# Decode cache values moved behind the state-space product of the output projection

## The chip, the cores and the metric

One core of a Trainium2 chip runs the whole kernel. The time is device microseconds from one execution to the end of it; a run's number is that of the core. The engines are TensorE (PE; its weight loads are PEld), VectorE (DVE), ScalarE (ACT), GpSimd (POOL) and SyncE (SP), whose queue issues nearly all DMAs in order. Each engine works its instructions off in the order in which they stand in the built program.

## The reference, cut to what matters

One step of a one-layer hybrid decoder: 1024 prompt tokens and 8 decode tokens (T = 1032 columns), model width 1024. Three attention patterns (dilated windows, 8 heads of 64 each) are merged per position by their softmax denominators; a Mamba-2 branch gives 1024 more columns, gated by silu(z) and normalised; one output projection takes both.

```python
def merge_patterns(outs, lses):
    alpha = jax.nn.softmax(jnp.stack(lses, axis=0), axis=0)
    o = sum(alpha[g][..., None] * outs[g] for g in range(N_PATTERNS))
    return o.reshape(o.shape[:-2] + (ATTN_OUT,))
...
    # decode tokens: each pattern's probabilities times the cached values
    o = jnp.einsum('bthk,btkhd->bthd', p, sel[:, :, :, 1].astype(jnp.float32)) / den
...
    ssm = ssd_gate_out(y, xs, z, d_skip, ssd_norm_w)
    mix = jnp.concatenate([attn.astype(xn.dtype), ssm.astype(xn.dtype)], axis=-1) @ w_out
```

The moved block computes that einsum over 128 cached keys for 8 decode tokens and 3 patterns, already weighted for the merge, and adds the new keys' part.

## The kernel before

Activations stand transposed, 128 rows of features by T columns, and the columns are cut into three chunks of 344 (688 to 1031, with the 8 decode tokens, is the last). Every large product is made of three fp32r products (high by high, high by low, low by high); load_w loads a 512 KB weight tile wr, ScalarE casts it to wh, and DVE (or GpSimd) subtracts to get wl. gemm does one weight tile against the chunks of cc: unit issues 8 x 3 matmuls of 128x344 per chunk into a PSUM tile g, about 7.5 us for two chunks.

A scheduler places the instructions of each engine when the program is built. The blocks carry priorities (the context prio): "evac" goes first, then "w" (weight loads and casts), "side", "late", and "main" (the matmuls of unit) last; inside one kind the order of the text counts. What has been placed on an engine runs in that order on the chip.

The stages around the change, in time:

- The z projection (the loop over k with gemm of w_in[36 + k], 831 to 976 us). Per k: 72 matmuls into g, ScalarE copies g to zt (L893), silu, DVE multiplies into yg (L901), ScalarE squares into zt (L906), and GpSimd adds the squares up in acc (L908, k = 1 to 6). k = 7's squares go straight to a matmul.
- Beside it, as "late" work: the merge weights. The softmax statistics come back as sn (L809), wg and wo are worked out, transposed (wtp), copied to wts (L834) and stored to w_d (L835).
- Then the merge of the prompt's attention, 16 rounds (4 quarters of the prompt by 4 head pairs, L838 to L849): load nt (384 KB, L840) and wt (2 broadcasts of 96 KB, L843), GpSimd multiplies (L845), DVE adds twice (L846, L847), ScalarE casts into ah (L848), DVE subtracts into al (L849). The pool mgp has two buffers of nt and of wt.
- Also "late" in the z stage: the decode block (L852 to L880). For each of 8 tokens, three loads of cached values (cvt, 128x512, 256 KB each, L861), three multiplies by probabilities (L864; pattern 0 on DVE, patterns 1 and 2 on GpSimd), two DVE adds (L867, L868), one matmul with a selector column (L869; sums over the 128 keys into nps, two records each). Then osb (copy, L871), four transposes (L874), adds into dat, and the last 8 columns of ah and al. The pool cvp has five buffers, so a token's three and two of the next fit.
- The state-space part of the output projection for chunks 0 and 1: the scaled rows sh and sl (L914, L915), the row sums (ptp, L921 and L922), then m = 0 and 1 in one loop (L945), then m = 2 to 7 by gemm with cc = (0, 1) (L953), evacuated by DVE into mix.
- The attention part, chunk 0 first (unit with ah, al and the pair of weights from load_pair, L959 on). The weights of m = 0, 1 and m = 2, 3 are kept in a pool wrs (wah0, wal0, wah2, wal2); later pairs are loaded again per chunk. Chunk 1 follows, and chunk 2, which alone reads the decode columns of ah and al.

The pools of the right-hand side of SBUF form a stack: a pool opened after another was closed takes its space, and its first writer waits for the last reader of what lay there. Before, mgp and cvp lie beside each other, both are closed, and wrs is opened in their space.

Of the kernel before, what the change touches and what calls it, by code (L numbers as in the profile page):

```python
# [8 lines left out]
F32 = mybir.dt.float32  # L9
# [39 lines left out]
def trunk(tc, a, o):  # L49
# [62 lines left out]
    def after(ins, first):  # L112
        tc.add_manual_dep(ins.ins, first.ins.name,
                          mybir.DependencyInfo(mybir.DependencyClass.Sync, mybir.DependencyReason.DATA),
                          reason="order")

    def next_copy(ins):
        pace[1] += pace[0]
        if copies and pace[1] >= 1:
            pace[1] -= 1  # L120
            d, s = copies.pop()
            after(nc.sync.dma_start(out=d, in_=s), ins)
# [37 lines left out]
    def unit(ps, w, hs, ls, c, ch=CH):  # L160
        wh, wl = w
        c0, c1 = ch[c]
        n = len(hs)
        with prio("main"):
            for k in range(n):
                ws = slice(k * P, (k + 1) * P)
                for j, (x, y) in enumerate(((wh, hs[k]), (wl, hs[k]), (wh, ls[k]))):
                    nc.tensor.matmul(ps, x[:, ws], y[:, c0:c1], start=(k == 0 and j == 0),  # L168
                                     stop=(k == n - 1 and j == 2))

    gpools = [psg]
    ngp = [0]
# [8 lines left out]
    def gemm(src, cols, hs, ls, evac, cc=(0, 1, 2), share=False):  # L181
        w = load_w(src, cols, share)
        for c in cc:
            ps = gps()
            unit(ps, w, hs, ls, c)
            with prio("evac"):
                next_copy(evac(c, ps))

    def rms(src_ps, dst):
        nc.scalar.activation(out=dst, in_=src_ps, func=AF.Sqrt, bias=epst, scale=1.0 / D)  # L190
# [607 lines left out]
    rst = ExitStack()  # L798
    mgp = pool(rst, "mgp", 2, side="right")
    QT = 256  # L800
    cvp = pool(rst, "cvp", 5, side="right")
    ah = cap.tile([P, HP, T], F32R, name="ah")
    al = cap.tile([P, HP, T], F32R, name="al")

# [43 lines left out]
                nc.scalar.copy(ah[:, hp, qs], nt[:, 0])  # L848
                nc.vector.tensor_tensor(out=al[:, hp, qs], in0=nt[:, 0], in1=ah[:, hp, qs], op=ALU.subtract)  # L849


    with prio("late"):  # L852
        sel = cap.tile([P, NB * NB], F32, name="sel")
        nc.vector.memset(sel, 0.0)
        nc.vector.memset(sel[:, 0:NB * NB:NB + 1], 1.0)
        ops = att_ps("nps")
        for b in range(NB):
            vts = []
            for g in range(NG):
                vt = cvp.tile([P, 512], F32, tag="cv", name="cvt")  # L860
                nc.sync.dma_start(out=vt, in_=a[f"cache{g}"][b].rearrange("(k r) c -> r k c", r=DIL[g])[0, :, 512:1024])  # L861
                pw = dpt[:, g].rearrange("p h (x b) -> p b x h", b=NB)[:, b].unsqueeze(3)
                v4 = vt.rearrange("p (x h d) -> p x h d", x=HP, h=2)
                (nc.gpsimd if g else nc.vector).tensor_tensor(out=v4, in0=v4, in1=pw.to_broadcast([P, HP, 2, 64]),  # L864
                                                              op=ALU.mult)
                vts.append(vt)
            nc.vector.tensor_tensor(out=vts[0], in0=vts[0], in1=vts[1], op=ALU.add)  # L867
            nc.vector.tensor_tensor(out=vts[0], in0=vts[0], in1=vts[2], op=ALU.add)  # L868
            nc.tensor.matmul(ops[:NB], sel[:, b * NB:(b + 1) * NB], vts[0], start=(b == 0), stop=(b == NB - 1))  # L869
        osb = cvp.tile([NB, 512], F32, tag="cv", name="osb")  # L870
        nc.scalar.copy(osb, ops[:NB])  # L871
        otp = att_ps("nps")
        for hp in range(HP):
            nc.tensor.transpose(otp[:, hp * NB:(hp + 1) * NB], osb[:, hp * P:(hp + 1) * P], ident[:NB, :NB])  # L874
        nc.vector.tensor_tensor(out=dat, in0=otp[:, 0:HP * NB], in1=dnv[:, 0], op=ALU.add)
        for g in range(1, NG):
            nc.vector.tensor_tensor(out=dat, in0=dat, in1=dnv[:, g], op=ALU.add)
        dv = dat.rearrange("p (h b) -> p h b", h=HP)
        nc.scalar.copy(ah[:, :, S:T], dv)
        nc.vector.tensor_tensor(out=al[:, :, S:T], in0=dv, in1=ah[:, :, S:T], op=ALU.subtract)  # L880
    rst.close()


# [4 lines left out]
    for k in range(KT):  # L888
        zt = gp.tile([P, T], F32, tag="zt", name="zt")

        def ev(c, ps, zt=zt):
            c0, c1 = CH[c]
            return nc.scalar.copy(zt[:, c0:c1], ps)  # L893

        gemm(a["w_in"][36 + k], 1024, xh, xl, ev)
        with prio("side"):
            yt = mixp.tile([P, T], F32, tag="mix", name=f"yg{k}")
            nc.sync.dma_start(out=yt, in_=y_d[k])
        with prio("evac"):
            nc.scalar.activation(out=zt, in_=zt, func=AF.Silu)  # L900
            nc.vector.tensor_tensor(out=yt, in0=yt, in1=zt, op=ALU.mult)  # L901
            yg.append(yt)
            if k == 0:
                nc.scalar.activation(out=acc, in_=yt, func=AF.Square)
            else:
                nc.scalar.activation(out=zt, in_=yt, func=AF.Square)  # L906
                if k < KT - 1:
                    nc.gpsimd.tensor_tensor(out=acc, in0=acc, in1=zt, op=ALU.add)  # L908
    sh, sl = [], []
    with prio("evac"):  # L910
        for k in range(KT):
# [36 lines left out]
    with prio("evac"):  # L948
        for m in range(2):
            for c in range(2):  # L950
                ssm_ev(m)(c, pq[m][c])
    for m in range(2, KT):
        gemm(a["w_out"][m][:, 512:1536], 1024, sh, sl, ssm_ev(m), cc=(0, 1))  # L953
    ahs = [ah[:, k] for k in range(HP)]
    als = [al[:, k] for k in range(HP)]
    wrs = pool(right, "wrs", 1, side="right")
# [308 lines left out]
```

## Time and profile before

| | us |
|---|---|
| median of 3 runs | 1928.76 |
| lowest, highest | 1927.81, 1932.84 |
| the profiled execution | 1929.59 |
| its span (first to last instruction) | 1927.8 |
| TensorE busy in it | 1825.0 |
| decode block, first load to last matmul | 875.0 to 950.1 |
| last subtraction of the merge (al) | 1035.4 |
| attention part, first matmul | 1049.9 |

The profiled execution took 1.8 us more than its span, and 0.8 more than the median. In the rows below L-numbers are lines of the kernel before; "idle before" is the time that an engine stood still just before an instruction, with what released it. A timeline row may stand for several equal instructions (x2), and for SP its length counts the waiting within the row.

### The profile page before, as it was taken

To read this page: it belongs to the slowest core of one execution; us is meant where nothing else is said; L and a number is where in the kernel's file an instruction comes from. 1 tells how busy PE (TensorE), PEld (TensorE's weight loads), DVE (VectorE), ACT (ScalarE), POOL (GpSimd) and SP (SyncE) were. 2 spreads that over 40 slices of the span, in tenths; PEclk is the share of its full clock that TensorE was granted. 3 is DMA by queue.
4 is the path that set the end of the run, shared out by engine and by line. 5 is a ranking of instruction groups with operands and counts; after the bars stand their busy time and mean duration, and the time that the engine had idled before them with its cause. 6 is when DMAs were issued, how large, how long until landed. Compare 5 with 4: busy or idle time off the path is not lost. (4 is left out here: it accounts for less than half of the span.)

```text
span 1927.8 us, 29260 instructions
## 1 busy us (share of the span) xinstructions
PE 1825.0 (95%) x11727; PEld 1709.3 (89%) x11727; DVE 1014.0 (53%) x1896; ACT 739.2 (38%) x1388; POOL 394.5 (20%) x277
## 2 busy tenths in 40 slices
PE   8999989999999899998879989999999999999994
PEld 6999878888888798887679989999999999999993
DVE  6544676757764544455774896331333333333348
ACT  5543554545554455665242353222221112211242
POOL 0000244543232311133533342000000000000025
PEclk9999999999999999999889999999999999999997
DMA  4322333443334433464754454347433643366362
GB/s 162 122 95 86 119 108 112 137 128 107 104 115 136 156 100 110 142 237 137 178 154 133 147 168 132 109 150 249 133 115 130 240 164 131 105 202 207 115 247 88
DMA packets 125544, 275.26 MB, mean 143 GB/s; under 512 B 17616, under 2 KB 83632, under 8 KB 124000
## 3 DMA queue, kind: packets, MB, share of 16 engines
q1 hardware_dynamic: 125408, 273.39, 43.4%
q8 instruction: 92, 1.51, 0.3%
q14 instruction: 44, 0.36, 0.1%
HBM read 235.86 MB, written 125.47 MB: 187 GB/s over the span
## 5 line engine op out<-in xcount | busy, mean ns | idle before, releaser
L168 PE MATMUL g<-xh,wh 128*128 128x344 f32 x1344 | 443.7, 330 | 9.7 <-ACT zt L893 5.5
L168 PE MATMUL g<-xl,wh 128*128 128x344 f32 x1344 | 440.4, 328 | 1.5 <-DVE xl L222 1.5
L168 PE MATMUL g<-xh,wl 128*128 128x344 f32 x1344 | 439.0, 327 | 0.5 <-DVE wl L157 0.5
L168 PEld LDWEIGHTS g<-xh,wh 128*128 128x128 f32 x1344 | 255.8, 190 | 19.3 <-ACT zt L893 6.1
L168 PEld LDWEIGHTS g<-xh,wl 128*128 128x128 f32 x1344 | 256.2, 191 | 11.3 <-issue 9.9
L168 PEld LDWEIGHTS g<-xl,wh 128*128 128x128 f32 x1344 | 256.3, 191 | 10.4 <-issue 7.4
L157 DVE TENSOR_TENSOR wl<-wr,wh 128x1024 fp32r<-128x1024 f32 (+1 forms) x133 | 163.0, 1226 | 124.9 <-ACT wh L156 124.7
L156 ACT CAST wh<-wr 128x1024 fp32r<-128x1024 f32 (+1 forms) x133 | 134.4, 1011 | 214.5 <-PE g L168 128.8
L168 PE MATMUL pg<-fh,wl 128*128 128x344 f32 x504 | 161.8, 321 | 0.2 <-DVE wl L157 0.2
L168 PE MATMUL pg<-fl,wh 128*128 128x344 f32 x504 | 161.8, 321 | 0.0
L168 PE MATMUL pu<-fl,wh 128*128 128x344 f32 x504 | 161.6, 321 | 0.0
L168 PE MATMUL pu<-fh,wh 128*128 128x344 f32 x504 | 161.2, 320 | 0.0
L168 PE MATMUL pu<-fh,wl 128*128 128x344 f32 x504 | 160.8, 319 | 0.0
L168 PE MATMUL pg<-fh,wh 128*128 128x344 f32 x504 | 158.5, 322 | 0.0
L1110 POOL TENSOR_TENSOR ow<-wr,ow 128x512 fp32r<-128x512 f32 x8 | 11.1, 1407 | 674.9 <-ACT ow L1109 674.9
L168 PE MATMUL g<-hl,wh 128*128 128x344 f32 x432 | 138.0, 319 | 0.0
L168 PE MATMUL g<-hh,wl 128*128 128x344 f32 x432 | 137.6, 319 | 0.0
L168 PE MATMUL g<-hh,wh 128*128 128x344 f32 x432 | 137.3, 320 | 0.0
L230 DVE TENSOR_TENSOR u<-pu,rf 128x344 f32<-128x344 f32 x66 | 34.1, 516 | 195.5 <-PE pu L168 195.5
L650 ACT ACTIVATE sm<-sm,ngm 128x128 f32<-128x128 f32 (+1 forms) x192 | 84.9, 443 | 108.3 <-DVE ngm L646 106.2
L606 POOL TENSOR_TENSOR sw<-sw,sin 128x1032 f32<-128x1032 f32 x24 | 74.9, 3122 | 247.6 <-ACT sw L605 184.1
L1079 ACT CAST hh<-s 128x344 fp32r<-128x344 f32 x66 | 31.7, 480 | 199.4 <-DVE s L1078 197.3
(323 smaller groups left out, 3710.7 us busy)
## 6 DMA issues: line engine op xcount, KB each, us to landing
out_skv<-in_cache SPq DMA_DIRECT2D x64, 1023.5 KB, 5.3
wr<-in_w_in SPq DMA_DIRECT2D x56, 512.0 KB, 3.8
wr<-in_w_fin SPq DMA_DIRECT2D x44, 512.0 KB, 3.8
out_skv<-in_cache SPq DMA_DIRECT2D x16, 1022.0 KB, 5.5
wr<-in_w_out SPq DMA_DIRECT2D x24, 512.0 KB, 4.1
wr<-in_w_fout SPq DMA_DIRECT2D x24, 384.0 KB, 4.2
e<-cs_d SPq DMA_DIRECT2D x16, 512.0 KB, 3.9
n_d<-nh SPq DMA_DIRECT2D x12, 512.0 KB, 4.2
```

Source lines behind the costliest of these rows:

```text
L156: nc.scalar.copy(wh[:, :cols], wr[:, :cols])
L157: nc.vector.tensor_tensor(out=wl[:, :cols], in0=wr[:, :cols], in1=wh[:, :cols], op=ALU.subtract)
L168: nc.tensor.matmul(ps, x[:, ws], y[:, c0:c1], start=(k == 0 and j == 0), stop=(k == n - 1 and j == 2))
L230: return nc.vector.tensor_tensor(out=dst, in0=ps, in1=r[:dst.shape[0], c0:c1], op=ALU.mult)
L606: nc.gpsimd.tensor_tensor(out=sw[:, 0:T], in0=sw[:, 0:T], in1=sin, op=ALU.mult)
L650: nc.scalar.activation(out=sm[:, h, :nk], in_=sm[:, h, :nk], func=AF.Exp, scale=SCALE, bias=ngm[:, g, j, i:i + 1], accum_out=den[:, g, j, ...
L1079: nc.scalar.copy(hh[:, c0:c1], s)
L1110: nc.gpsimd.tensor_tensor(out=wl, in0=src, in1=wh, op=ALU.subtract)
```

## The change

Three things. (1) The decode block goes, in the text, from behind the merge to behind the state-space products of m = 2 to 7, and its pool cvp is now opened there, after mgp has been closed. It keeps the "late" priority. Since wrs is opened after cvp is closed, mgp, cvp and wrs now follow each other in the same space. (2) Two dependencies without a semaphore pin TensorE's order: the first cvt matmul not before the last matmul of m = 4 (done[2]), the first transpose not before the last of m = 6 (done[4]). unit and gemm return their last matmul for that. (3) The sum of squares of k = 6 is added by DVE and not by GpSimd.

```diff
+    def behind(ins, prev):
+
+        tc.add_manual_dep(ins.ins, prev.ins.name,
+                          mybir.DependencyInfo(mybir.DependencyClass.NoSync, mybir.DependencyReason.DATA),
+                          reason="order")
...
     mgp = pool(rst, "mgp", 2, side="right")
     QT = 256
-    cvp = pool(rst, "cvp", 5, side="right")
...
-    with prio("late"):
...
-        ops = att_ps("nps")
-        for b in range(NB):
...
     rst.close()
...
-                    nc.gpsimd.tensor_tensor(out=acc, in0=acc, in1=zt, op=ALU.add)
+                    (nc.gpsimd if k < KT - 2 else nc.vector).tensor_tensor(out=acc, in0=acc, in1=zt, op=ALU.add)
...
+    done = []
     for m in range(2, KT):
-        gemm(a["w_out"][m][:, 512:1536], 1024, sh, sl, ssm_ev(m), cc=(0, 1))
+        done.append(gemm(a["w_out"][m][:, 512:1536], 1024, sh, sl, ssm_ev(m), cc=(0, 1)))
+
+    rst = ExitStack()
+    cvp = pool(rst, "cvp", 5, side="right")
+    with prio("late"):
+        sel = cap.tile([P, NB * NB], F32, name="sel")
+        nc.vector.memset(sel, 0.0)
+        nc.vector.memset(sel[:, 0:NB * NB:NB + 1], 1.0)
+        ops = att_ps("nps")
+        for b in range(NB):
+            vts = []
+            for g in range(NG):
+                vt = cvp.tile([P, 512], F32, tag="cv", name="cvt")
+                nc.sync.dma_start(out=vt, in_=a[f"cache{g}"][b].rearrange("(k r) c -> r k c", r=DIL[g])[0, :, 512:1024])
+                pw = dpt[:, g].rearrange("p h (x b) -> p b x h", b=NB)[:, b].unsqueeze(3)
+                v4 = vt.rearrange("p (x h d) -> p x h d", x=HP, h=2)
+                (nc.gpsimd if g else nc.vector).tensor_tensor(out=v4, in0=v4, in1=pw.to_broadcast([P, HP, 2, 64]),
+                                                              op=ALU.mult)
+                vts.append(vt)
+            nc.vector.tensor_tensor(out=vts[0], in0=vts[0], in1=vts[1], op=ALU.add)
+            nc.vector.tensor_tensor(out=vts[0], in0=vts[0], in1=vts[2], op=ALU.add)
+            ins = nc.tensor.matmul(ops[:NB], sel[:, b * NB:(b + 1) * NB], vts[0], start=(b == 0), stop=(b == NB - 1))
+            if b == 0:
+                behind(ins, done[2])
+        osb = cvp.tile([NB, 512], F32, tag="cv", name="osb")
+        nc.scalar.copy(osb, ops[:NB])
+        otp = att_ps("nps")
+        for hp in range(HP):
+            ins = nc.tensor.transpose(otp[:, hp * NB:(hp + 1) * NB], osb[:, hp * P:(hp + 1) * P], ident[:NB, :NB])
+            if hp == 0:
+                behind(ins, done[4])
+        nc.vector.tensor_tensor(out=dat, in0=otp[:, 0:HP * NB], in1=dnv[:, 0], op=ALU.add)
+        for g in range(1, NG):
+            nc.vector.tensor_tensor(out=dat, in0=dat, in1=dnv[:, g], op=ALU.add)
+        dv = dat.rearrange("p (h b) -> p h b", h=HP)
+        nc.scalar.copy(ah[:, :, S:T], dv)
+        nc.vector.tensor_tensor(out=al[:, :, S:T], in0=dv, in1=ah[:, :, S:T], op=ALU.subtract)
+    rst.close()
     ahs = [ah[:, k] for k in range(HP)]
     als = [al[:, k] for k in range(HP)]
     wrs = pool(right, "wrs", 1, side="right")
```

What it does to the order of the engines. TensorE in the z stage, before: g_9157 is a chunk of the z projection, nps the decode block's sum.

```order
L168 MATMUL g_9157<-xh0_112,wl_9101 128x344
L168 MATMUL g_9157<-xl0_120,wh_9100 128x344
L168 MATMUL g_9157<-xh1_113,wh_9100 128x344
L869 MATMUL nps_8622<-cvt_8623,sel_8619 8x512
L869 MATMUL nps_8622<-cvt_8635,sel_8619 8x512
L869 MATMUL nps_8622<-cvt_8647,sel_8619 8x512
L168 MATMUL g_9157<-xh1_113,wl_9101 128x344
L168 MATMUL g_9157<-xl1_121,wh_9100 128x344
```

In the changed kernel no row of nps from cvt stands among the z matmuls. Its first one stands where the product of m = 7 begins (g_9784 is chunk 1 of m = 6, g_9816 chunk 0 of m = 7; TensorE, changed kernel):

```order
L174 MATMUL g_9784<-sh7_9373,wh_9753 128x344
L174 MATMUL g_9784<-sh7_9373,wl_9754 128x344
L174 MATMUL g_9784<-sl7_9374,wh_9753 128x344
L952 MATMUL nps_9874<-cvt_9875,sel_9871 8x512
L174 MATMUL g_9816<-sh0_9345,wh_9811 128x344
L174 MATMUL g_9816<-sh0_9345,wl_9812 128x344
```

The second and third stand within m = 7, and five in a row behind its last matmul, right ahead of the attention part (TensorE, changed kernel; g from sh and sl is chunk 1 of m = 7, g from ah the attention part):

```order
L174 MATMUL g<-sh_9373,wh 128x344
L174 MATMUL g<-sh_9373,wl 128x344
L174 MATMUL g<-sl_9374,wh 128x344
L952 MATMUL nps<-cvt,sel 8x512 x5
L959 MATMUL nps<-ident,osb 128x8 x4
L174 MATMUL g<-ah,wah_9987 128x344 x2
L174 MATMUL g<-ah,wah_9993 128x344 x2
L174 MATMUL g<-ah,wal_9988 128x344
L174 MATMUL g<-al,wah_9987 128x344
L174 MATMUL g<-ah,wah_9987 128x344
```

Here the transposes of osb moved in front of the attention part's first matmuls as well. SP's queue at the start of the merge, before (sn are the statistics, nt and wt a merge round, w_d the store of the merge weights):

```order
L809 DMA sn_8426<-st_d_346 128x8x16
L840 DMA nt<-n_d 128x3x256 x2
L861 DMA cvt<-in_cache 128x512 x6
L835 DMA w_d<-wts 64x3x128
L861 DMA cvt<-in_cache 128x512
L843 DMA wt<-w_d 64x3x256 x2
L141 DMA wr<-in_w_out 128x1024
L843 DMA wt<-w_d 64x3x256 x2
```

In the changed kernel the six cvt loads ahead of the w_d store, and all others of that stretch, are gone; they stand at the end of the merge (nt is the sixteenth round's load, wr of 128x2x512 the weights of the attention part's pairs; SP, changed kernel):

```order
L147 DMA wr<-in_w_out 128x1024
L850 DMA wt<-w_d 64x3x256 x2
L847 DMA nt<-n_d 128x3x256
L982 DMA wr<-in_w_out 128x2x512
L944 DMA cvt<-in_cache 128x512 x5
L982 DMA wr<-in_w_out 128x2x512
L944 DMA cvt<-in_cache 128x512 x19
L982 DMA wr<-in_w_out 128x2x512 x4
L147 DMA wr<-in_w_out 128x1024 x2
```

The loads of all pairs but the first now stand behind cvt loads, where before six of them followed the last nt in a row. ScalarE at the end of the merge, before and then changed (wah_9987 is the first pair's high half, wah_9993 the second's):

```order
L156 CAST wh<-wr 128x1024 x2
L848 CAST ah<-nt 128x256 x2
L156 CAST wh<-wr 128x1024
L848 CAST ah<-nt 128x256
L969 CAST wah_9987<-wr 128x1024
L156 CAST wh<-wr 128x1024
L969 CAST wah_9993<-wr 128x1024
L969 CAST wh<-wr 128x1024 x2
L982 ACTIVATE nacc<-mix_9512 128x344
```

```order
L162 CAST wh<-wr 128x1024
L855 CAST ah<-nt 128x256 x2
L162 CAST wh<-wr 128x1024
L855 CAST ah<-nt 128x256
L162 CAST wh<-wr 128x1024
L956 COPY osb<-nps 8x512
L984 CAST wah_9987<-wr 128x1024
L984 CAST wah_9993<-wr 128x1024
L966 CAST ah<-dat 128x4x8
```

In the second, the copy of osb, the end of the decode block's sum, stands ahead of both casts of wah. On DVE the last al of the merge now stands behind the first evacuation of m = 5, and the adds of the decode block behind that al.

## Rows read from the trace of the kernel before

**Rows 1.** The profile page: busy us, share, instructions of each engine.

```profile
PE 1825.0 (95%) x11727; PEld 1709.3 (89%) x11727; DVE 1014.0 (53%) x1896; ACT 739.2 (38%) x1388; POOL 394.5 (20%) x277
```

**Rows 2.** Groups, 870 to 1056 us: busy us, mean ns, idle before.

```profile
L168 PE MATMUL g<-xh,wh 128*128 128x344 f32 x133 | 44.1, 331 | 5.5 <-ACT zt L893 5.5
...
L869 PE MATMUL nps<-cvt,sel 128*8 128x512 f32 x16 | 8.7, 649 | 7.3 <-DVE cvt L868 6.3 <-PE g L168 1.0
...
L921 PE MATMUL ptp<-acc,ones 128*128 128x344 f32 x6 | 2.3, 470 | 2.4 <-POOL acc L908 2.4
```

**Rows 3.** Windows: us, busy by engine (instructions), granted TensorE clock, DMA share, GB/s.

```profile
876.00:976.00 100.00, 81.21 (x437) 68.55 (x436) 65.77 (x88) 36.31 (x62) 46.70 (x29) 0.93 0.64 170
998.00:1051.00 53.00, 48.80 (x301) 47.13 (x301) 29.78 (x42) 11.51 (x17) 16.68 (x8) 1.00 0.52 156
1051.00:1071.00 20.00, 20.00 (x127) 19.78 (x127) 11.97 (x17) 6.39 (x11) 7.19 (x3) 1.00 0.25 79
```

**Rows 4.** Timeline of TensorE behind a wait at 858 us: start, duration (us).

```profile
857.95 0.39 PE L744 MATMUL stp<-ident,scs 128*32 128x128 f32 x2 [1.99 <-DVE scs L740]
...
859.26 0.49 PE L168 MATMUL g<-xl,wh 128*128 128x344 f32 x1
...
862.41 0.41 PE L168 MATMUL g<-xh,wl 128*128 128x344 f32 x1
```

**Rows 5.** Tile wah: count, ns min/median/max, first and last start (us).

```profile
L168 PE MATMUL g<-ah,wah x16: 316/320/322, 1049.9 to 1057.0; 128*128 128x344 f32 x16
```

**Rows 6.** Timeline of DVE at the end of the merge.

```profile
1035.43 0.43 DVE L849 TENSOR_TENSOR al<-nt,ah 128x256 fp32r<-128x256 f32 x1
```

**Rows 7.** Timeline of SP's queue, 905 to 918 us (issues, waiting included).

```profile
906.62 10.45 SPq L861 DMA_DIRECT2D cvt<-in_cache  x6
917.17 0.61 SPq L835 DMA_DIRECT2D w_d<-wts  x1
```

**Rows 8.** Timeline of ScalarE at 910 and 1035 us.

```profile
910.72 0.47 ACT L834 COPY wts<-wtp 64x384 f32<-64x384 f32 x1 [2.52 <-PE wtp L832]
...
1035.89 1.05 ACT L969 CAST wah<-wr 128x1024 fp32r<-128x1024 f32 x1 [0.49 <-DVE al L849]
```

**Rows 9.** Timeline of GpSimd, 925 to 1040 us [idle before, releaser].

```profile
926.37 1.84 POOL L845 TENSOR_TENSOR nt<-nt,wt 128x768 f32<-128x768 f32 x1 [3.56 <-DMA wt<-w_d]
...
954.20 1.83 POOL L845 TENSOR_TENSOR nt<-nt,wt 128x768 f32<-128x768 f32 x1 [2.37 <-DMA nt<-n_d]
957.08 1.85 POOL L845 TENSOR_TENSOR nt<-nt,wt 128x768 f32<-128x768 f32 x1 [1.04 <-DVE nt L847]
965.78 1.84 POOL L845 TENSOR_TENSOR nt<-nt,wt 128x768 f32<-128x768 f32 x1 [6.85 <-DMA nt<-n_d]
...
978.38 1.80 POOL L845 TENSOR_TENSOR nt<-nt,wt 128x768 f32<-128x768 f32 x1 [6.03 <-DMA nt<-n_d]
...
1032.13 1.85 POOL L845 TENSOR_TENSOR nt<-nt,wt 128x768 f32<-128x768 f32 x1 [7.53 <-DMA nt<-n_d]
1037.07 2.43 POOL L970 TENSOR_TENSOR wal<-wr,wah 128x1024 fp32r<-128x1024 f32 x1 [3.08 <-ACT wah L969]
```

**Rows 10.** Tile cvt: count, ns min/median/max, first and last start (us).

```profile
L861 SPq DMA_DIRECT2D cvt<-in_cache x24: 327/427/631, 875.0 to 937.8; - x24
L864 POOL TENSOR_TENSOR cvt<-cvt,dpt x16: 1057/1142/1513, 880.4 to 943.4; 128x512 f32<-128x512 f32 x16
...
L867 DVE TENSOR_TENSOR cvt<-cvt x8: 677/1534/1545, 881.5 to 944.8; 128x512 f32<-128x512 f32 x8
L868 DVE TENSOR_TENSOR cvt<-cvt x8: 677/688/1537, 884.5 to 948.5; 128x512 f32<-128x512 f32 x8
...
DMA to landing us min/median/max: 2.6/4.7/7.5
```

**Rows 11.** Tile osb: count, ns min/median/max, first and last start (us).

```profile
L874 PE MATMUL nps<-ident,osb x4: 202/202/225, 956.7 to 956.9; 8*128 8x8 f32 x4
L871 ACT COPY osb<-nps x1: 569/569/569, 952.8 to 952.8; 8x512 f32<-8x512 f32 x1
```

More of the change, by code (lines that the diff above doesn't have):

```diff
@@ L167, in unit @@
                 for j, (x, y) in enumerate(((wh, hs[k]), (wl, hs[k]), (wh, ls[k]))):
-                    nc.tensor.matmul(ps, x[:, ws], y[:, c0:c1], start=(k == 0 and j == 0),
-                                     stop=(k == n - 1 and j == 2))
+                    last = nc.tensor.matmul(ps, x[:, ws], y[:, c0:c1], start=(k == 0 and j == 0),
+                                            stop=(k == n - 1 and j == 2))
+        return last
     gpools = [psg]
@@ L184, in gemm @@
             ps = gps()
-            unit(ps, w, hs, ls, c)
+            last = unit(ps, w, hs, ls, c)
             with prio("evac"):
                 next_copy(evac(c, ps))
+        return last
     def rms(src_ps, dst):
@@ L849, in trunk @@
                 nc.vector.tensor_tensor(out=al[:, hp, qs], in0=nt[:, 0], in1=ah[:, hp, qs], op=ALU.subtract)
-    with prio("late"):
-        sel = cap.tile([P, NB * NB], F32, name="sel")
-        nc.vector.memset(sel, 0.0)
-        nc.vector.memset(sel[:, 0:NB * NB:NB + 1], 1.0)
-        ops = att_ps("nps")
-        for b in range(NB):
[L858 to L880, printed above, removed]
     rst.close()
```

## The prediction

> **What bounds the kernel now.** I read the page first: TensorE is busy for 95% of the span, DVE for 53 and the others for less [rows 1], so time is won only where TensorE waits or runs slowly, and lost wherever a new wait is put in front of it. Next the groups of instructions between 870 and 1056 us: the matmuls that the change moves (tile nps from cvt) took 8.7 us and stood behind 7.3 us of idle time, 6.3 of it until the second DVE add of a batch; the z matmuls behind them lost another 5.5 to ScalarE's copies, and the row sums at the end 2.4 to GpSimd's last add into acc [rows 2]. Then three windows: in the 100 us of the z stage in which the decode block runs, TensorE is busy for 81.2 and its granted clock is 0.93; in the attention part from 1051 on it is busy throughout at 1.00 [rows 3]. So the z stage has some room, and the place to which the block goes has none: whatever comes late at 1050 moves the end of the kernel one to one.
>
> **Part 1, taken out of the z stage: a gain of 22 us for TensorE there.** Its matmuls and their waits go: 8.7 + 7.3 = 16.0 us [rows 2]. A granted clock of 0.93 over 100 us means that about 14 us passed at half clock (1.2 of 2.4 GHz) [rows 3], and a matmul there follows the last one after 0.29 us (11 steps between 859.26 and 862.41 [rows 4]) in place of 0.157 (20.00 us over 127 matmuls [rows 3]); that is up to 7 us lost. The waits that went before these stretches are only partly those of the block, so I take 5, with 0 and 7 as ends. The add of k = 6 goes from GpSimd to DVE: it can't win more than the 2.4 us wait [rows 2], and at worst the DVE add queues as long; I take 1. Together 22 us (16 to 26). The m = 7 product of the state-space part, 48 matmuls before the attention part's first at 1049.9 [rows 5], begins at 1049.9 - 48 x 0.157 = 1042.4 now and could begin at about 1020.
>
> **Part 2, the merge ahead of it.** This decides when the moved block can start: its five buffers lie where the merge had its own, so the first load waits for the last subtraction into al, which now ends at 1035.43 + 0.43 = 1035.9 [rows 6]. How much earlier will that be? The store of the merge weights stands behind six cvt loads on SP: these held the queue for 10.45 us from 906.62, the store went at 917.17 although ScalarE had the weights at 911.2 [rows 7, 8]. Without them it goes 6.0 earlier; the state loads in front of it also stood behind cvt loads, and I add 1. So the first merge round starts at 926.37 - 7 = 919.4 [rows 9]. From the first to the sixteenth round it took 1032.13 - 926.37 = 105.8 us, 14.1 for two rounds (there are two buffers) [rows 9]. In the best stretch two rounds took 11.58 and 12.60 (954.20, 965.78, 978.38) [rows 9]; GpSimd, without 16 cvt multiplies of 1.14 us [rows 10], and with TensorE's results drawn off earlier, should keep to that, 12.1. Fifteen steps are 7.5 x 12.1 = 90.8, and from the last multiply to the last al it is 3.7: 919.4 + 90.8 + 3.7 = 1014. Ends: at the old pace 1029; and not under 1003 to 1008, because that al now stands on DVE behind the first evacuation of m = 5, which TensorE can't finish earlier than one and a half products (8.4 us each, 53 us over 301 matmuls x 48 [rows 3]) before m = 7. So the merge ends some 6 us before TensorE comes to m = 7, 22 before it is where it was.
>
> **Part 3, the block in its new place.** Here is the cost. TensorE's first cvt matmul stands right in front of m = 7, the next two within it, five in a row behind it, then the transposes. A batch takes three of five buffers, so from the second batch on a load waits for an add of the batch before. One turn is: issue 0.43, landing, one GpSimd multiply 1.14, one DVE add 0.69 [rows 10]. Landing was 2.6 at least, 4.7 in the middle, 7.5 at most [rows 10]; with at most five loads of 256 KB under way and the merge's loads over, I take 3.0, nearer to the low end. That gives 5.3 a batch (4.9 by the low end, 7.0 by the middle, 9.8 by the highest). In the z stage the block was spread over some 70 us and hidden behind z matmuls; now only m = 7 lies beside it, 7.5 us of work. First batch: three issues 1.3, landing 3.0, two multiplies 2.3, two adds 1.4, 8.0 in all. So the last batch is added up at 1014 + 8 + 7 x 5.3 = 1059.1.
>
> **Part 4, from there to the attention part.** The weights of its first pair (wah0, wal0) are now placed in the space that the cvt buffers give up, so their cast, which today stands right behind the last al and runs at 1035.89 [rows 8], long before it is needed, waits for the end of the block. Behind the last add come one batch's matmul 0.6 [rows 2], the copy of the sums 0.57, four transposes 0.4 [rows 11], the cast 1.05 [rows 8] and GpSimd's subtraction for wal0 2.43 [rows 9]: 5.1 us. Only four matmuls can go ahead of wal0. The attention part runs from about 1064.2 and not from 1049.9: 14.3 later. TensorE will have idled for most of 25 to 30 us in front of it, so it starts at the lower clock; by the twelve or so slow steps after the wait at 858 [rows 4], 12 x 0.13 = 1.6 us more. The loads of the later pairs stand behind all cvt loads on SP; they have 5 us of matmuls per pair to hide under, and I cost them at nothing. If that cover fails it is one landing, 4 us.
>
> **The sum.** The z stage's 22 us is not seen, since the chain of Part 3 ends later than TensorE would: +14.3 + 1.6 = +15.9 against the profiled run of 1929.59, which is 0.8 above the median of the runs: 1945.5 there, 1945 as a median. The forecast's own ends: 1003 with 4.9 a batch gives 1003 + 42.3 + 5.1 = 1050.4, +2; 1014 with 7.0 gives 1076, +28.
>
> **A rule beside the rows.** The adds of this chain took 0.68 us or 1.54 [rows 10], two values and little between them. The Trainium skill, "SBUF — State Buffer", section "SBUF: two separate sides", says that a VectorE instruction with two SBUF inputs and a GpSimd one lock each other out of a shared port for a whole instruction. The rows agree with it in that the longer value is about one GpSimd multiply above the shorter. By it the multiplies of the next batch would fall into the adds of this one and a turn would be 0.85 longer, 1951 in all; by the lower value it is the 1945 above. I keep the lower because a turn here is mostly the wait for a load, during which GpSimd has nothing to do.
>
> **Rivals.** (a) *The gain survives, faster.* The merge, freed of cvt loads and multiplies, would have to end by about 996, which is 10.0 us for two rounds in place of 12.1 (919.4 + 75 + 3.7 = 998), and the turn stay at 4.9: 996 + 42.3 + 5.1 = 1043.4, with the clock's 1.6 five under today, 1924; every microsecond of merge under that counts fully. For it: two rounds stood 2.9 us apart where both buffers were full (954.20 and 957.08 [rows 9]). Against: the last merge round stands behind m = 5 on DVE, so TensorE would also have to gain over 30 us in the z stage. About 1921. (b) *The two cancel, no change.* Merge at its floor of 1003 and turns of 4.9: 1931 from the sum above; the point is a last al at 1000 to 1004. (c) *Loads as slow as they were.* Landing 4.7 as in the middle row: +28, 1957. For it: 24 loads of the same shape on the same queue; against: those landed beside the merge's, the state's and the weights' loads. (d) *The change doesn't do what it says.* The pins hold only a lower bound (not ahead of m = 4, not ahead of m = 6), and the order already shows the cvt matmuls further back than that. Without them TensorE would wait in other places but the chain of Part 3 would end at the same time: 1945 again.
>
> **How the numbers follow.** A measurement of this kernel can tell about 0.3%, 5.8 us, from no change. (a) has 0.12, (b) with all that lies between 1923 and 1934.5 has 0.14, my forecast and (d) 0.50, (c) and the worse ends 0.24. So faster 0.12, same 0.14, slower 0.74. Time 1945. The range goes from 1925, which takes in (b) and leaves (a) out, to 1961, which takes in (c) and leaves out only a merge at its old pace with slow loads as well: about 0.2 outside.
>
> **What would show it.** Right: no idle time before nps in the z stage and z matmuls at a clock of 1.00 there; the last al near 1014; cvt loads issued one batch at a time from then on, 5 us apart; on TensorE a gap of 25 us or more around m = 7 that ends with DVE's second add or with wal0; the attention part beginning near 1064 at the lower clock. Wrong, if cvt loads land before the last al, if the wait at m = 7 is under 10 us, or if the merge ends before 1000.

## The result and the profile after

The changed kernel is slower: 1956.82 us (median of 4 runs, 1954.13 to 1957.91) against 1928.28 for the kernel before in the same comparison, a ratio of 1.0142 (95% interval 1.0122 to 1.0162), 28.5 us. The forecast was 1945 with 1925 to 1961 around it. The profiled execution took 1956.65, with a span of 1954.9, 27.1 more than that of before.

The page, and TensorE's waits from 870 to 1090 us (line, releaser: us in total, times, longest):

```profile
PE 1836.0 (94%) x11727; PEld 1716.7 (88%) x11727; DVE 1015.4 (52%) x1897; ACT 738.3 (38%) x1388; POOL 389.9 (20%) x276
```

```profile
PE nps L952 <- DVE cvt L951: 13.5, 6, 3.9
PE g L174 <- ACT zt L870: 6.8, 3, 4.2
...
PE nps L952 <- issue: 4.8, 1, 4.8
```

The wait of the cvt matmuls for the second add has not gone. Where 6.3 us of it stood in the z stage [rows 2], 13.5 now stand between 1030 and 1068, and 4.8 more at the first of them (the profile names no releaser for it; the add that it needed ended at 1034.06, and it began at 1034.16). Windows over the stretches of [rows 3]:

```profile
876.00:976.00 100.00, 87.89 (x526) 83.85 (x527) 53.01 (x81) 47.46 (x75) 26.03 (x13) 0.93 0.42 116
998.00:1051.00 53.00, 45.82 (x256) 40.43 (x254) 31.15 (x42) 5.93 (x9) 20.21 (x14) 0.94 0.55 170
1051.00:1071.00 20.00, 8.09 (x12) 0.91 (x12) 10.18 (x12) 0.57 (x1) 7.55 (x8) 0.55 0.37 111
```

The z stretch holds 526 matmuls where it held 437: TensorE does more there. Its granted clock is 0.93 as before; the 1.00 that was named as a sign of being right did not come. The stretch from 1051 to 1071, full before with 127 matmuls, now has 12 and a clock of 0.55. The block itself, as the tile cvt (to set beside [rows 10]):

```profile
L944 SPq DMA_DIRECT2D cvt<-in_cache x24: 327/328/433, 1024.6 to 1061.5; - x24
L947 POOL TENSOR_TENSOR cvt<-cvt,dpt x16: 1056/1060/1788, 1028.4 to 1065.4; 128x512 f32<-128x512 f32 x16
...
L950 DVE TENSOR_TENSOR cvt<-cvt x8: 677/1527/1543, 1030.5 to 1065.5; 128x512 f32<-128x512 f32 x8
L951 DVE TENSOR_TENSOR cvt<-cvt x8: 679/686/1551, 1033.4 to 1067.1; 128x512 f32<-128x512 f32 x8
...
  ACT osb L956: 44.7, 1
...
DMA to landing us min/median/max: 2.7/3.1/4.5
```

The first load is issued at 1024.6 and the last lands after 1064; from the first load to the last add the block takes 43 us, where it was spread over 74 [rows 10], and the copy of its sums waits 44.7 us for it. The chain in time, on four engines: GpSimd's first and last merge multiply, DVE's last al and the second adds of the first and the last batch, SP's cvt loads, then TensorE.

```profile
916.73 1.84 POOL L852 TENSOR_TENSOR nt<-nt,wt 128x768 f32<-128x768 f32 x1 [12.75 <-DMA wt<-w_d]
...
1020.85 1.86 POOL L852 TENSOR_TENSOR nt<-nt,wt 128x768 f32<-128x768 f32 x1 [5.37 <-DMA nt<-n_d]
```

```profile
1024.15 0.42 DVE L856 TENSOR_TENSOR al<-nt,ah 128x256 fp32r<-128x256 f32 x1
...
1033.38 0.68 DVE L951 TENSOR_TENSOR cvt<-cvt 128x512 f32<-128x512 f32 x1
...
1067.08 0.69 DVE L951 TENSOR_TENSOR cvt<-cvt 128x512 f32<-128x512 f32 x1
```

```profile
1024.61 2.25 SPq L944 DMA_DIRECT2D cvt<-in_cache  x5
...
1032.02 29.81 SPq L944 DMA_DIRECT2D cvt<-in_cache  x19
```

```profile
1049.41 1.02 PE L952 MATMUL nps<-cvt,sel 128*8 128x512 f32 x2 [1.59 <-DVE cvt L951]
1054.34 1.88 PE L952 MATMUL nps<-cvt,sel 128*8 128x512 f32 x2 [3.90 <-DVE cvt L951]
1059.12 1.88 PE L952 MATMUL nps<-cvt,sel 128*8 128x512 f32 x2 [2.91 <-DVE cvt L951]
1063.48 1.88 PE L952 MATMUL nps<-cvt,sel 128*8 128x512 f32 x2 [2.48 <-DVE cvt L951]
1067.83 1.87 PE L952 MATMUL nps<-cvt,sel 128*8 128x512 f32 x2 [2.47 <-DVE cvt L951]
1070.41 0.59 PE L959 MATMUL nps<-ident,osb 8*128 8x8 f32 x4 [0.71 <-ACT osb L956]
1072.18 1.89 PE L174 MATMUL g<-ah,wah 128*128 128x344 f32 x4 [1.18 <-ACT wah L984]
1074.65 0.66 PE L174 MATMUL g<-ah,wal 128*128 128x344 f32 x1 [0.58 <-POOL wal L985]
...
1080.26 0.33 PE L174 MATMUL g<-ah,wah 128*128 128x344 f32 x1
```

The loads begin when the last al is written (1024.15 + 0.42, and the first load at 1024.61), as the shared space demands. SP's queue is held by the other 19 for 29.8 us. From 1054 on TensorE meets a batch every 4.4 to 4.9 us, each after 2.5 to 3.9 us of waiting and at the lower clock (1.87 us for what took 1.02 at 1049.41), then the transposes, wah and wal. The attention part begins at 1072.18 with four matmuls and in earnest at 1074.65, against 1049.9 [rows 5]; up to 1080.26 its matmuls follow each other at 0.29 us, at a granted clock of 0.50, the lower level of 1.2 GHz. The waits from 1029.3 to there are no single gap of 25 us: they are ten, 20.8 us together.

### The profile page after: what moved, and what is told of

It is laid out like the page before. It is cut to its first block, busy times and chain, and to the rows that moved or that the text cites. A ratio compares the mean times of both kernels' runs of the same rounds, so it can differ in the third digit from the quotient of the medians.

```text
span 1954.9 us, 29273 instructions
## 1 busy us (share of the span) xinstructions
PE 1836.0 (94%) x11727; PEld 1716.7 (88%) x11727; DVE 1015.4 (52%) x1897; ACT 738.3 (38%) x1388; POOL 389.9 (20%) x276
```

## The experiments

The profiled executions differ by up to 10 us before the z stage is reached, where the programs run the same instructions. So this table gives times from a common mark, the first load of yg (SP's queue, at 847.6 in the kernel before, 849.8 in the changed one). "Merge" is the way from the first to the last of GpSimd's 16 merge multiplies, "attention" the first matmul of the attention part, "end" the end of the span. The ratios come from the timed runs.

| kernel | ratio to before (95% interval) | merge, us | attention after mark | end after mark |
|---|---|---|---|---|
| before | 1 | 105.8 | 202.3 | 1080.2 |
| changed | 1.0142 (1.0122 to 1.0162) | 104.1 | 222.4 | 1105.1 |
| noblock | 0.9942 (0.9927 to 0.9956) | 105.5 | 188.2 | 1068.5 |
| noblock_p | 0.9924 (0.9898 to 0.9950) | 100.4 | 184.0 | 1060.1 |
| acconly | 1.0041 (1.0025 to 1.0056) | 105.1 | 209.4 | 1088.1 |
| moveonly | 1.0125 (1.0097 to 1.0152) | 99.4 | 217.4 | 1097.7 |
| cv9 | 1.0081 (1.0064 to 1.0098) | 104.7 | 214.1 | 1094.4 |
| own3 | 1.0172 (1.0145 to 1.0199) | 104.0 | 228.0 | 1111.0 |
| late | 1.0147 (1.0134 to 1.0160) | 105.1 | 191.4 | 1105.8 |
| mg3 | 1.0078 (1.0053 to 1.0104) | 82.8 | 207.3 | 1087.8 |
| mg3cv9 | 1.0010 (0.9996 to 1.0024) | 85.2 | 204.8 | 1082.4 |
| pinz | 1.0008 (0.9995 to 1.0021) | 105.5 | 202.7 | 1079.6 |

With both pins taken out, the built program has the same order of instructions, row for row. They bind nothing, since the scheduler put the matmuls further back than they ask.

**noblock and noblock_p: what the block costs at all.** The changed kernel without the block, with the k = 6 add on DVE and on GpSimd.

```diff
-        for b in range(NB):
...
-        nc.vector.tensor_tensor(out=dat, in0=otp[:, 0:HP * NB], in1=dnv[:, 0], op=ALU.add)
+        nc.vector.tensor_copy(dat, dnv[:, 0])
```

> The changed kernel with the decode block left out: no cvt load, multiply, add or matmul, and no copy of osb; the decode columns of the merged attention come from the new keys alone. All else as in the changed kernel, the k = 6 add on DVE too. My theory: what the move took out of the z stage is worth what TensorE had in hand at m = 7 in the changed kernel, 1042.4 - 1029.3 = 13 us, and the chain behind the merge cost the rest. So the attention part should begin near 1037 and the time be about 1916, 40 under the changed kernel. If the merge itself now held TensorE (its last al was at 1024.6 in the changed kernel), the attention part could not begin before about 1030 either, which changes nothing. Rival: the z stage never gave anything, then 1926 to 1930.

> The changed kernel without the decode block (its decode columns come from the new keys alone) and with the k = 6 add back on GpSimd: the kernel before without the block, in other words. It gives what the block costs in its old place. The kernel without the block and with the add on DVE had a ratio to before of 0.9942. Theory A, the add costs 8 us here as well: 0.990. Theory B, it cost 8 only by the order it caused there: 0.994. The terms of my sum gave the z stage 21 us without the add (1910, 0.989), of which 13 were seen at m = 7 in the changed kernel.

Measured: 1918.44 against 1930.80 before, and 1913.41 against 1929.02. So the block costs 12 to 16 us in its old place, with what goes with it there, and 39 in the new one (1.0142 - 0.9942 = 0.020 of 1930). The z stage does give something; behind the merge the block costs two and a half to three times as much. Of the 12 to 16 us, 8.7 are its own matmuls [rows 2], which go with it to any place: a move could win some 4 to 7. The intervals of the two runs overlap, so they don't settle what the add on DVE costs without the block. The merge, though, is hardly quicker without the block. Its 16 multiplies, noblock first:

```profile
L852 POOL TENSOR_TENSOR nt<-nt,wt x16: 1800/1844/3442, 913.0 to 1018.5; 128x768 f32<-128x768 f32 x16
```

```profile
L852 POOL TENSOR_TENSOR nt<-nt,wt x16: 1797/1852/2807, 914.9 to 1015.3; 128x768 f32<-128x768 f32 x16
```

It starts 11 to 13 us earlier than the 926.37 of [rows 9], but takes 105.5 and 100.4 us to the last multiply. The block was not what set its pace, and this is the term in which the sum failed.

**mg3: what sets the pace of the merge.** The changed kernel with the k = 6 add on GpSimd and a third buffer.

```diff
-    mgp = pool(rst, "mgp", 2, side="right")
+    mgp = pool(rst, "mgp", 3, side="right")
```

> The changed kernel with the k = 6 add on GpSimd, and three buffers for the merge instead of two. In nine kernels so far the merge's sixteen rounds took 99 to 106 us from first to last multiply, with the decode block beside them, behind them or left out; so it was not the block that set the pace, which is where my sum failed. Theory A: the pace is the way of a buffer (load, multiply, two adds, cast, subtraction, next load) twice over, and a third buffer brings the rounds to about 80 us: the last al near 1000, the chain behind it ends 17 us earlier, the attention part near 1050, and the time that of the kernel before: ratio 1.000. Theory B: the pace is set by the evacuations and weight casts that stand among the merge on DVE, or by SP's queue: 99 us again, ratio 1.0125.

```profile
L852 POOL TENSOR_TENSOR nt<-nt,wt x16: 1799/1854/2336, 918.4 to 1001.2; 128x768 f32<-128x768 f32 x16
```

82.8 us, where moveonly, the same kernel with two buffers, takes 99.4: theory A. With two buffers a merge round waits for its own buffer's way through load, multiply, adds, cast and subtraction. The rest also follows: the first cvt load is at 1006.2 (1019.0 with two buffers), and the attention part begins 10.1 us earlier after the mark than in moveonly. The ratio came to 1.0078, not 1.000, as the last al stood at 1006 and not at 1000 and the chain behind it took 48.6 us (1006.2 to 1054.8) in place of 43.2 (43.1 in moveonly). Why it took longer there was not tried.

**cv9: what sets the turn of the chain.** The changed kernel with nine cvt buffers.

```diff
-    cvp = pool(rst, "cvp", 5, side="right")
+    cvp = pool(rst, "cvp", 9, side="right")
```

> The changed kernel with nine cvt buffers and not five, in the same space behind the merge. My theory: a turn of the chain (4.8 us a batch between the second adds) is mostly the wait of a load for a buffer and its landing. With nine buffers three batches load at once, and a batch should cost about 3.2 us: 7 x 1.6 = 11 us less, 1946. Rival (bandwidth of the loads or GpSimd's multiplies set the turn): GpSimd needs 2.2 us a batch, so it alone could not; 6.3 MB at the 160 to 170 GB/s seen there would take 38 us, and the time would stay at 1955 to 1957.

```profile
L944 SPq DMA_DIRECT2D cvt<-in_cache x24: 327/364/433, 1024.5 to 1051.5; - x24
...
L952 PE MATMUL nps<-cvt,sel x16: 592/596/1061, 1035.0 to 1059.3; 128*8 128x512 f32 x16
```

1947.22 against 1930.80: 1.0081, 12 us under the changed kernel's ratio. The first cvt matmul to the last took 24.3 us (1035.0 to 1059.3) in place of 34.4 (1034.2 to 1068.6), 3.5 a batch. A batch's turn was the wait of its loads for buffers, as the forecast had it; neither GpSimd's multiplies nor the loads' bandwidth held it at 4.8.

**mg3cv9: both together.** Three merge buffers and nine cvt buffers, the k = 6 add on GpSimd.

```diff
-    mgp = pool(rst, "mgp", 2, side="right")
+    mgp = pool(rst, "mgp", 3, side="right")
...
-    cvp = pool(rst, "cvp", 5, side="right")
+    cvp = pool(rst, "cvp", 9, side="right")
```

> As the kernel with three merge buffers, and nine cvt buffers too (there is room for both, as one pool follows the other). Nine buffers alone brought the chain from 43 us to 34 behind the last al. If the merge ends near 1000 (theory A above), the chain ends near 1034 and the attention part begins when TensorE is through with m = 7, near 1035 to 1040: 10 to 15 us faster than before, ratio 0.993. If the merge keeps its pace (theory B), 1.006, what nine buffers gave alone less the add on DVE.

1931.40 against 1930.25, no difference that can be told. From moveonly, which differs in the two pools alone, it is 22 us (1.0125 to 1.0010); the third merge buffer alone gave 9 and the nine cvt buffers alone 12. So the two waits account for the loss, and taking them away gives it back, but no more. The expected gain on top of it stayed out since TensorE did not reach the end of m = 7 before 1058 there. Its attention part begins 20.8 us later after the mark than that of noblock_p. Of these, 5.2 are lost by the last copy of z (106.6 us after the mark, 101.4 in noblock_p), some 8 are the block's eight pairs of matmuls at 1.02, and 4.5 the waits for its adds; the rest stays open. DVE is full between 1020 and 1040, but TensorE waited there for cvt adds alone; its last wait for a low half of the weights ended at 1010.71, before the block's first add:

```profile
1010.71 0.66 PE L174 MATMUL g<-sh,wl 128*128 128x344 f32 x1 [3.21 <-DVE wl L163]
PE nps L952 <- DVE cvt L951: 4.5, 4, 2.6
1020.00:1040.00 20.00, 16.66 (x71) 11.22 (x71) 19.91 (x20) 1.88 (x2) 14.63 (x12) 0.91 0.71 236
```

**own3: is it the shared space?** Three cvt buffers beside the merge's own, so that no cvt load waits for the last al.

```diff
     mgp = pool(rst, "mgp", 2, side="right")
     QT = 256
+    cvp = pool(rst, "cvp", 3, side="right")
...
-    rst = ExitStack()
-    cvp = pool(rst, "cvp", 5, side="right")
```

> The changed kernel with three cvt buffers in a space of their own beside the merge's (there is room for three only) in place of five in the merge's space, so that no cvt load waits for the merge's end. My theory: the first load's wait for the last al made the chain late. Now loads start in the z stage; with three buffers a batch takes some 8 to 9 us, but most batches are done by the end of the merge, and what is left behind it is about three: the attention part near 1055, a ratio of 1.005. Rival: the place in the order alone makes it late (DVE and GpSimd serve the merge first), 1.014; or SP's queue, held by cvt loads again, makes the merge late as before, 1.010 or more.

1.0172 and no better than the changed kernel (the intervals overlap). The loads did start at 872.5, but GpSimd's order has only two batches before the merge and the other six behind its last multiply:

```profile
892.92 1.06 POOL L945 TENSOR_TENSOR cvt<-cvt,dpt 128x512 f32<-128x512 f32 x1 [3.41 <-DMA cvt<-in_cache]
...
1021.27 1.84 POOL L853 TENSOR_TENSOR nt<-nt,wt 128x768 f32<-128x768 f32 x1 [6.09 <-DMA nt<-n_d]
1023.07 2.25 POOL L945 TENSOR_TENSOR cvt<-cvt,dpt 128x512 f32<-128x512 f32 x2
```

```profile
PE nps L950 <- DVE cvt L949: 22.1, 4, 7.5
```

With three buffers a batch took 6.6 us at the end (1055.89, 1062.46, 1069.10 on TensorE), and the 22.1 us of waits for adds are more than the 18.3 of the changed kernel. So the shared space is not the whole cause: the place in the order makes the block last on GpSimd, whatever its space, and fewer buffers make the chain slower. Five buffers in a space of their own stay untried: there is room for three only.

**acconly and moveonly: the add on DVE.** The kernel before with only that edit, and the changed kernel without it.

```diff
-                    nc.gpsimd.tensor_tensor(out=acc, in0=acc, in1=zt, op=ALU.add)
+                    (nc.gpsimd if k < KT - 2 else nc.vector).tensor_tensor(out=acc, in0=acc, in1=zt, op=ALU.add)
```

> The kernel before with only the k = 6 add of squares moved from GpSimd to DVE. My theory priced this at 1 us at most: 1926 to 1929, no difference that can be told. Rival: the add on DVE queues behind the merge's adds and holds the row sums, 1932 or more.

> The changed kernel with its third part undone: the k = 6 add of squares back on GpSimd, the block and the pins as changed. Alone, that add on DVE cost 8 us in the kernel before (ratio 1.0041). Theory A, the parts add up: 8 us less than the changed kernel, a ratio to before of about 1.010. Theory B: alone it cost 8 us because it gave the state-space part another order, in which DVE's low half for one product came 5.8 us late; in the changed kernel the wait behind the merge hides such a thing, and the ratio stays at 1.014.

1938.84 against 1930.80 for the edit alone: 8 us slower, where 1 us was expected either way. TensorE's waits, and DVE at the longest of them:

```profile
PE g L168 <- DVE wl L157: 6.5, 2, 5.8
...
PE ptp L921 <- DVE acc L908: 4.9, 1, 4.9
```

```profile
1013.20 0.42 DVE L846 TENSOR_TENSOR nt<-nt 128x256 f32<-128x256 f32 x1 [1.90 <-POOL nt L845]
1013.54 3.96 DVE L157 TENSOR_TENSOR wl<-wr,wh 128x1024 fp32r<-128x1024 f32 x2
```

The wait for the sum did not shrink but doubled (2.4 [rows 2], now 4.9), and 5.8 us fell on TensorE at 1016.4, since the low half for a product of the state-space part stands behind a merge add that had itself waited 1.9 for GpSimd. In the order of the built program the edit also changes the order of that part's products on TensorE. In the changed kernel, undoing it gave 1.0125 after 1.0142; the intervals overlap, so this part's share there isn't settled, though the profile ends 7.4 us earlier after the mark and the merge takes 99.4 us in place of 104.1.

**late: further back.** The block behind the attention part of chunks 0 and 1, ahead of chunk 2, with the first pair of weights kept alone.

```diff
-    kept = {m: load_pair(m, True) for m in (0, 2)}
+    kept = {m: load_pair(m, True) for m in (0,)}
...
         if c == 2:
+            cst = ExitStack()
+            cvp = pool(cst, "cvp", 5, side="right")
...
+                    if b == 0:
+                        behind(ins, lastu)
```

> The decode block moved further, behind the attention part of chunks 0 and 1 and ahead of chunk 2, which alone reads its columns. Its first cvt matmul is pinned behind chunk 1's last attention matmul. For room, only the first pair of attention weights is kept (wah0, wal0); the second is loaded again per chunk like the others. wrs no longer lies behind the block, so wah0 need not wait for it. My theory: the z stage's 13 us survive and the block hides beside the attention part: about 1916, some 12 us faster than before. Rival: the block's matmuls wait again in their new place, or the weights loaded again come late: 1925 to 1940.

```profile
PE g L174 <- ACT ah L1005: 10.9, 1, 10.9
...
PE g L174 <- DVE mix L1014: 6.4, 2, 4.0
```

```profile
1120.00:1140.00 20.00, 16.88 (x89) 12.98 (x88) 20.00 (x21) 5.99 (x8) 12.16 (x9) 1.00 0.45 137
1140.00:1160.00 20.00, 9.14 (x42) 8.62 (x41) 19.46 (x29) 11.04 (x24) 11.14 (x9) 0.66 0.63 201
```

The attention part does begin early, 10.9 us before that of the kernel before after the mark. Everything is lost behind it: DVE has no room between 1120 and 1160, evacuations wait behind the block's adds, and chunk 2 waits 10.9 us for the decode columns. 1.0147, 1959.8 us: neither the theory's 1916 nor the rival's 1925 to 1940, but worse than both. The second pair of weights, loaded again per chunk here, was not tried apart from the place of the block.

**pinz: the old place, with pins that bind.** The block in the z stage as before, each cvt matmul from the fourth on held back to behind a later z unit.

```diff
+    ZP = {3: 15, 4: 16, 5: 17, 6: 19, 7: 21}
...
+            if b >= 3:
+                behind(ins, zd[ZP[b]])
```

> The decode block in its old place in the z stage (the pools and the order of before, the k = 6 add on GpSimd), with one thing of the change: pins. From the fourth batch on, each cvt matmul is pinned behind the z unit after the one in which it stood before, 24 matmuls or less later, when its adds are done. My theory: TensorE's 6.3 us of waiting for the second add go, and some of the stretches at half clock: 6 to 9 us faster than before, ratio 0.996. Rival: the buffers that the later matmuls hold delay the loads, and SP's queue with them the store of the merge weights; the merge ends later and the attention part waits for it: 1.000 or more.

```profile
PE g L174 <- ACT zt L873: 13.0, 3, 5.6
...
PE nps L907 <- DVE cvt L906: 1.4, 2, 0.9
```

1.0008, no difference, where 6 to 9 us had been expected. The waits of 6.3 us for the adds went to 1.4 (and 1.6 more without a named releaser), and those of the z matmuls for ScalarE's copies rose from 5.5 [rows 2] to 13.0. The rival's reason is not it: the last al stands 188.3 us after the mark, 187.8 before. The cvt matmuls, it seems, only stood where TensorE would have waited for something else.

No version beat the kernel before with its work complete.

## Why the prediction was right, and where its size was off

The direction was right, and so was the step that decides it, a chain behind the merge in front of TensorE. Two terms of the sum were not: the pace of the merge (Part 2) and, without weight for the time, the gain of the z stage (Part 1). Point by point:

- *What bounds the kernel*: a late start at 1050 moves the end one to one. The attention part in earnest moved by 24.6 us (1074.65, where its first matmul with wal stood at 1050.04), the end of the span by 27.1.
- *Part 1*, a z stage gain of 22 us at m = 7. TensorE stood at its first cvt matmul, right ahead of m = 7, from 1029.3 (1034.16 less the 4.8 of waiting), against 1042.4: 13.1, or 15.3 after the mark. noblock_p, which has no chain, has its attention part 18.3 earlier after the mark. The term was 7 to 9 us too big. By the last of ScalarE's copies of z, 17.9 us were won (110.1 us after the mark in place of 128.0), near the 16.0 of matmuls and waits; the 5 us put on the clock did not come, as it stayed at 0.93; and 2.6 were lost again before m = 7. It did not matter for the time, as the forecast said, since the chain ended later still. Its share for the add on DVE had the wrong sign: 8 us lost when alone.
- *Part 2*, the last al at 1014, was the term that failed. The first merge multiply was where it was put (916.73, forecast 919.4), but the step by which GpSimd, without the cvt multiplies, should keep to 12.1 us for two rounds did not hold: 104.1 us over fifteen steps, 13.9 for two. The last al came at 1024.6, 10.6 late. mg3 shows why: the rounds wait for their two buffers. The best stretch of before was not what a merge without the block does throughout. The rows of before said so: the block's last multiply on GpSimd starts at 943.4 [rows 10], the fourth merge multiply (shown below) right behind it, at 944.83. From the fifth to the sixteenth, 954.20 to 1032.13 [rows 9], with nothing of the block between them, eleven steps took 77.9 us, 14.2 for two.
- *Part 3*, the chain. From the first load to the last second add 43.2 us, forecast 45.1: the first batch 9.4 and not 8.0, seven turns of 4.8 and not 5.3. Landing was 3.1 us in the middle, taken as 3.0. This is the step that decided the sign, and it held; cv9 shows that the buffers set it.
- *Part 4*, from the last add to the attention part, 5.1 forecast; 6.9 measured (1067.77 to 1074.65), the matmul pair and the transposes at the lower clock. After it the clock cost 2.6 us (19 steps in 5.61 us from 1074.65 to 1080.26, 2.98 at 0.157), not 1.6.

The fourth merge multiply of before:

```profile
944.83 2.37 POOL L845 TENSOR_TENSOR nt<-nt,wt 128x768 f32<-128x768 f32 x1 [0.19 <-DMA nt<-n_d]
```

ScalarE's copies of z, before and changed:

```profile
L893 ACT COPY zt<-g x24: 418/439/450, 834.7 to 975.6; 128x344 f32<-128x344 f32 x24
L870 ACT COPY zt<-g x24: 418/445/448, 836.8 to 959.9; 128x344 f32<-128x344 f32 x24
```

The sum of the misses: +10.6 for the merge, -1.9 for the chain, +1.8 behind it, +1.0 for the clock, 11.5 in all; the forecast of 1945.5 for the profiled execution and the 1956.65 that came differ by 11.2. That the time lies in the range is in part luck: the upper end of 1961 was there for slow loads, and the time came near it by another way. Rival (c), slow loads, gave the measured time by the wrong way: landing did not go up to 4.7. Rival (d) was half true, the pins bind nothing, and cost nothing. Of the signs of being wrong, one is doubtful: TensorE's wait at the first cvt matmul, ahead of m = 7, was 4.8 us and not over 10; only with the waits in and behind m = 7 is it 20.8. Rivals (a) and (b) wanted the last al at or under 1004; only three merge buffers come near that.

The rule that was weighed beside the rows: the Trainium skill, "SBUF — State Buffer", section "SBUF: two separate sides", has a VectorE instruction with two SBUF inputs and a GpSimd one that reads SBUF lock each other out for a whole instruction. In the changed kernel five of the eight first adds and one of the second took some 1.53 us, the others 0.68. Each long one began while a GpSimd multiply ran, and no short one did; one pair:

```profile
1044.97 1.22 POOL L947 TENSOR_TENSOR cvt<-cvt,dpt 128x512 f32<-128x512 f32 x1 [0.24 <-DMA cvt<-in_cache]
1045.20 1.54 DVE L950 TENSOR_TENSOR cvt<-cvt 128x512 f32<-128x512 f32 x1
```

The rows agree with the rule, and the choice of the shorter value was wrong for the first add and right for the second. The turn was shorter than forecast all the same, 4.8 for 5.3, so not every part of it was sized rightly.

What stays open: how much the add on DVE costs within the changed kernel (0 to 7 us), and which of the stretches between the z stage and m = 7 give back 4 to 8 us of the z stage's gain even without the block (from the last z copy to the attention part it is 74.3 us before, 78.1 in noblock and 82.6 in noblock_p).

## What to carry to other kernels

A pool that takes over a closed pool's space inherits its end: before moving a block, ask who last reads the space, and who will wait for the block's own space in turn; here the merge, the block and the next weights became one chain. Beside the work of the z stage the block cost 12 to 16 us, most of it its own matmuls; as a chain in front of an idle TensorE it cost 39. And a pace read from the best stretch of a loop is a guess as long as it isn't known what sets it; counting the way of one buffer would have told more than taking away a neighbour.

## What was not expected of the hardware

A single add, put on DVE, where it takes 1.2 us and not GpSimd's 2.4, cost 8 us in the kernel before: by the profile through the order of other things on DVE and TensorE and not by its own length.
